# Gate gathers in front of their rows, POOL's share of the splits kept to the end, and the lists' one-hots by one comparison on the vector engine

## The chip, the cores and the metric

The kernel runs on one core of one Trainium2 chip. The metric is the device time of one execution in microseconds (us). Three timed runs of the kernel before gave 2374.19, 2374.76 and 2380.31 us; the median is 2374.76 us. The engines are named as in the profile: PE multiplies matrices (PEld is its loading of weights), DVE is the vector engine, ACT the scalar engine, POOL the GpSimd engine, which also issues all gathers by index, and SP issues plain transfers.

## The reference

One layer on 256 latent tokens and 256 context tokens of width 2048, in float32: modulated RMSNorm, one input projection, a bidirectional mLSTM and a differential attention, gated sum, output projection, residual; then a retrieval of experts, and a final RMSNorm. Only the retrieval matters here, cut to its core:

```python
def peer(h, w_pq, sub_keys, expert_u, expert_v):
    q = (h @ w_pq).reshape(B, T, P_HEADS, 2, P_KEY_DIM // 2)
    s = jnp.einsum('bthpd,hpnd->bthpn', q, sub_keys)
    s1, i1 = lax.top_k(s[..., 0, :], P_TOPK)       # 16 of 128 keys
    s2, i2 = lax.top_k(s[..., 1, :], P_TOPK)
    ...                                             # the best 16 of their 256 sums
    g = jax.nn.softmax(top_s, axis=-1)
    def block(args):                                # 16384 experts, 8 x 16 for each token
        hx, ix, gx = args
        act = jax.nn.gelu(jnp.einsum('td,ted->te', hx, expert_u[ix]))
        return jnp.einsum('te,ted->td', gx * act, expert_v[ix])
```

Each token has 8 heads of 16 experts. An expert is one row of 2048 numbers in `expert_u` and one in `expert_v`, 16384 of each (128 MB a matrix).

## The kernel before

A product in full precision is made of three products of halves. `stage` (line 126) loads a piece of 128x1024 numbers (`raw`), ACT rounds it (`hi`, line 133), and DVE or POOL subtracts (`lo`, line 136). While the flag `by_four` is set, every fourth `lo` goes to POOL and three to DVE; once the flag `alone` is set too, all go to DVE. `raw`, `hi` and `lo` have three buffers each, so a piece is made at most three ahead of its use.

The last half of the program is the retrieval. Its stages overlap:

- **The u stage.** For each of 128 columns of experts, PE multiplies the tokens with `expert_u` (`u_pair`, two columns a call). A column is two half columns, and a half column is one piece: 8 products with `hi` (512 wide) and 8 with `lo` (256 wide). DVE then adds the two halves (`act`, line 1601), ACT takes the gelu (line 1602), and the result is written to `ag_dram` (line 1606), where each expert has its activations beside its gate weights.
- **Side work.** At each half column, `pump` takes `pace[0]` steps of a generator (`plan`): the selection of experts, the map of gate weights (`gate_map`), the lists of experts by the group of tokens that uses them (`lists`), and the first row groups (`soon`). A tile scheduler puts the instructions of each engine in an order; the gathers and the matmuls of this stage keep the order of the program. Every engine works its own order through without leaving it.
- **`lists`** ends with 126 columns of places. For four columns at a time `one_hots` makes two tiles: `o1`, one-hots of the place inside a block, on ACT (an Abs for each column, a Relu for four), and `o2`, one-hots of the block times the expert's number, by four comparisons, two on DVE and two on POOL (line 1238). PE multiplies them (the matmuls `g<-o,o`) and sums 126 products in one PSUM tile. From it come `idxV` and `idxG`, the lists for the gathers.
- **The v stage.** Experts come in blocks of 128. For each block POOL gathers 128 rows of `expert_v` (`vraw`, 1 MB, `stage_rows`) and 128 rows of gates and activations from `ag_dram` (`ag`, 128 KB for one token tile, 256 KB for two, `stage_gates`); DVE multiplies gate and activation (`w`, lines 1509 and 1512). A block used by all tokens of a tile is split into `hi`, `lo` (lines 1488, 1490, 1496, 1497) and multiplied in 12 matmuls for each token tile; blocks that 32 tokens use come by fours (an item) and are multiplied unsplit, 32 columns each (`v<-vraw,w`). There are 99 gathered blocks and 2 plain ones (`DENSE`). `soon` takes the first five items of four while the u stage still runs and fetches two more; the rest are worked off after it.

Rows come in tiles of two: four tiles at first, and two more (`vex`) once the u stage has given up its memory, so 12 rows. A tile is filled again when both of its rows have been multiplied. Gates have buffers of their own, 8 of 128x256 and 4 of 128x512. `fetch_gates` issues them up to five items ahead as far as these buffers go, item by item, and `next_item` issues it before and after the rows.

Of the kernel before, what the change touches and what calls it, by code (L numbers as in the profile page):

```python
# [19 lines left out]
F32 = mybir.dt.float32  # L20
# [65 lines left out]
def build(tc, a, dump=None):  # L86
# [34 lines left out]
    rings = []  # L121

    shared = [0]
    alone = [False]

    def stage(src, ring=None):
        if ring is None:
            ring = rings.pop(0)
            rings.append(ring)
        pool, bufs = ring  # L130
        r = load(src, pool, bufs[0])
        h = pool.tile([P, 1024], F32R, name="hi", tag="hi", bufs=bufs[1])
        nc.scalar.copy(h, r)  # L133
        l = pool.tile([P, 1024], F32R, name="lo", tag="lo", bufs=bufs[2])
        shared[0] = (shared[0] + 1) % 4 if by_four[0] and not alone[0] else 1
        (nc.vector if shared[0] else nc.gpsimd).tensor_tensor(l, r, h.bitcast(F32), op=OP.subtract)  # L136
        return h, l

# [31 lines left out]
    def b3(t, n):  # L170
        return t.unsqueeze(2).to_broadcast([P, t.shape[1], n])
# [1058 lines left out]

    def one_hots(rows, cols, factor, n=4, width=P):
        o1 = gm.tile([P, 4, P], F32, name="o1", tag="o1", bufs=3)
        for i in range(n):
            nc.scalar.activation(o1[:, i], iota, AF.Abs, bias=rows[:, i:i + 1], scale=-1.0)
        nc.scalar.activation(o1[:, 0:n], o1[:, 0:n], AF.Relu, bias=ones[:, 0:1], scale=-1.0)
        o2 = gm.tile([P, 4, P], F32, name="o2", tag="o2", bufs=3)
        for i in range(n):
            (nc.gpsimd if i % 2 else nc.vector).tensor_scalar(o2[:, i, 0:width], iota[:, 0:width], cols[:, i:i + 1], factor[:, i:i + 1],  # L1238
                                    op0=OP.is_equal, op1=OP.mult)
        return o1, o2  # L1240
# [49 lines left out]
    def lists():  # L1290
# [99 lines left out]
            w = slice(i, min(i + 4, N_LIST))  # L1390
            return one_hots(hl[:, 1, w], hl[:, 0, w], number[:, w], w.stop - i, N_BLOCKS)

        pace[0] = 1.05
        ready = [hots(0)]
        yield
        ready.append(hots(4))
# [23 lines left out]
        ls.release()  # L1420
        yield

    vst = None
    pace = [1.05]

    def plan():
        nonlocal vst
        yield from retrieve(0)
        for _ in weave(gate_map(0), retrieve(1)):
            yield  # L1430
        tk.release()
        vst = tc.alloc_tile_pool(name="vst", bufs=1, side="right", reuse_waits="tile")
        yield from gate_map(1)
        while leaving:
            step(leaving)
            yield
        pace[0] = 2
        yield from lists()
        pace[0] = 1.3
        alone[0] = True  # L1440
        yield from soon()

    n = P - N_LIST + 1
# [33 lines left out]
    def stage_gates(kind, i):  # L1477
        if kind == DENSE:
            return i
        n = len(TILES[kind])  # L1480
        ag = vst.tile([P, 2 * n * P], F32, name="ag", tag=f"ag{n}", bufs=AG[n - 1])
        src = (ag_tile, ag_dram)[n - 1]
        gather(ag, src[0:2 * P * (1 + EARLY)] if kind < 8 and i < CAPS[kind] - 1 else src, idxG, BASE[kind] + i)
        return {t: ag[:, 2 * j * P:2 * (j + 1) * P] for j, t in enumerate(TILES[kind])}
# [29 lines left out]
        return out  # L1514

    FIRST_OF = [sum(len(x) for x in ITEMS[:n]) for n in range(len(ITEMS) + 1)]
    rows_in = []
    gates_in = []
    staged = [0, 0]


    AG = 8, 4
    USES = [[sum(k != DENSE and len(TILES[k]) == w for k, _ in x) for w in (1, 2)] for x in ITEMS]

    def fetch_gates(n):
        while staged[1] < (min(len(ITEMS), n + 5) if n else 1) and all(sum(u[w] for u in USES[n:staged[1] + 1]) <= AG[w] for w in range(2)):
            gates_in.append([stage_gates(*b) for b in ITEMS[staged[1]]])
            staged[1] += 1

    def next_item(n):  # L1530
        if n > 1:
            fetch_gates(n)
        while staged[0] < len(ITEMS):
            last = FIRST_OF[staged[0] + 1] - 1
            if last // 2 * 2 - 11 >= FIRST_OF[n] or vex is None and last > 7:
                break
            rows_in.append([stage_rows(*b) for b in ITEMS[staged[0]]])
            staged[0] += 1
        fetch_gates(n)
        return [(raw, weights_of(kind, ins)) for (kind, _), raw, ins in  # L1540
                zip(ITEMS[n], rows_in.pop(0), gates_in.pop(0))]

    def accumulators(t):
        pool = tc.alloc_tile_pool(name=f"psV{t}", bufs=1, space=PSUM, side=("left", "right")[t], reuse_waits="tile")
# [16 lines left out]
    def soon():  # L1561
        nonlocal psG
        psG.release()
        out_acc[0] = accumulators(0)
        work = SOON + ITEMS[:2]
        for n, item in enumerate(work):
            rows, gates = [], []
            if n == 0:
                rows = [stage_rows(*b) for b in item]
                while made[0] < EARLY:  # L1570
                    yield
            for j, b in enumerate(item):
                if n:
                    rows.append(stage_rows(*b))
                    yield
                gates.append(stage_gates(*b))
                if j == 1 and 0 < n <= len(SOON):
                    parts = [(raw, weights_of(kind, ins)) for (kind, _), raw, ins in zip(work[n - 1], *held)]
                yield
            if 0 < n <= len(SOON):  # L1580
                v_groups(0, work[n - 1], parts, first=n == 1)
                yield
            held = rows, gates
            if n >= len(SOON):
                rows_in.append(rows)
                gates_in.append(gates)
                staged[0] += 1
                staged[1] += 1

    back.append(plan())  # L1590
    pump(1)
# [56 lines left out]
    with tc.If(rest > 0):  # L1648
        with tc.For_i(0, N_LIST, 1) as i:
            col_ = av.tile([P, 1], F32, name="ocol", bufs=1)  # L1650
            nc.sync.dma_start(col_, over_dram[:, bass.ds(i, 1)])
            for t in range(2):
                ag = av.tile([P, 2 * P], F32, name="oag", bufs=1)
                nc.sync.dma_start(ag, ag_dram[bass.ds(i * P + P, P), 2 * t * P:2 * (t + 1) * P])
                w = av.tile([P, P], F32, name="ow", bufs=1)
# [53 lines left out]
            residual(t, c)  # L1709
    for t in range(2):  # L1710
        finish_tile(t)
    for p in (fn, vex, *v_pools, av, vst, tkr, gm, stg, cst, dr):
        p.release()


# [67 lines left out]
```

## Time and profile before

| | before |
|---|---|
| median of 3 runs | 2374.76 us |
| profiled execution | 2391.27 us, span 2389.6 us |
| PE busy | 2240.4 us (94%) |
| DVE, ACT, POOL busy | 1540.9, 1101.3, 904.9 us |
| granted TensorE clock, mean | 0.973 |
| u stage, first to last matmul | 1176 to 2079 us |
| the lists' one-hots | about 1792 to 1908 us |
| first row gather | 1913 us |
| v stage after the u stage | 2079 to 2366 us |

How to read it: times in rows count from the start of the span. A row in order of time gives start and length in us, engine, line, operation, the tile written and the tiles read (numbers left out), its shape, and in brackets how long the engine had been idle and what ended that. PE's rows overlap, since matmuls are pipelined: the distance of two starts is what one costs.

### The profile page before, as it was taken

Reading aid. Unit: us, or ns where it says so; the run is one execution under the profiler, and the core shown is the slowest. Engines: PE = TensorE matmul, PEld = TensorE weight load, DVE = VectorE, ACT = ScalarE, POOL = GpSimd, SP = SyncE. Lnnn points to the kernel's source line nnn. Section 1 sums busy time; section 2 is a strip of 40 time slices with the busy share of each in tenths; the row PEclk is TensorE's granted clock in tenths of the full one; section 3 lists DMA queues with packets and bytes.
Section 4 is the critical chain, followed back from the end, with each engine's and each line's share of the span. In section 5 each row is a group of like instructions: output and inputs, shape, how many; then the busy total and the mean of one; then the engine's idle time right before and its main releaser. Section 6 shows DMA issues by size and latency. Waiting matters only on the chain. (4 is left out here: it accounts for less than half of the span.)

```text
span 2389.6 us, 37883 instructions
## 1 busy us (share of the span) xinstructions
PE 2240.4 (94%) x14330; PEld 1920.6 (80%) x14330; DVE 1540.9 (64%) x2898; ACT 1101.3 (46%) x1849; POOL 904.9 (38%) x908
## 2 busy tenths in 40 slices
PE   6999999999999999999998999999999989988786
PEld 3679989998889999879987888887889967665553
DVE  3357874768866768656798667874985434444444
ACT  3232322244556644444445778973338723333332
POOL 2132211245624200002266556752227642454554
PEclk9999999999999999999999999999999999999898
DMA  9968954876546588755555578789555589886977
GB/s 380 348 203 317 322 207 167 300 206 173 150 127 196 200 280 282 254 194 165 178 178 181 176 208 221 202 224 262 174 185 170 160 330 359 333 344 253 381 299 268
DMA packets 235913, 571.02 MB, mean 239 GB/s; under 512 B 85154, under 2 KB 118739, under 8 KB 221264
## 3 DMA queue, kind: packets, MB, share of 16 engines
q1 hardware_dynamic: 153888, 339.34, 43.9%
q0 software_dynamic: 46992, 211.67, 24.7%
q10 hardware_dynamic: 34848, 17.57, 2.5%
q8 instruction: 113, 1.85, 0.3%
q14 instruction: 72, 0.59, 0.1%
HBM read 524.33 MB, written 38.93 MB: 236 GB/s over the span
## 5 line engine op out<-in xcount | busy, mean ns | idle before, releaser
L133 ACT CAST hi<-raw 128x1024 fp32r<-128x1024 f32 x528 | 552.3, 1049 | 806.0 <-PE acc L289 270.0
L136 DVE TENSOR_TENSOR lo<-raw,hi 128x1024 fp32r<-128x1024 f32 x467 | 588.8, 1265 | 268.2 <-ACT hi L133 261.6
L92 PE MATMUL s<-h,hi 128*128 128x512 f32 x2048 | 748.3, 407 | 1.7 <-ACT hi L133 1.7
L92 PE MATMUL s<-h,lo 128*128 128x256 f32 x2048 | 581.5, 284 | 30.4 <-DVE lo L136 26.1
L92 PEld LDWEIGHTS s<-h,hi 128*128 128x128 f32 x2048 | 391.1, 191 | 96.0 <-ACT hi L133 5.2
L92 PEld LDWEIGHTS s<-h,lo 128*128 128x128 f32 x2048 | 393.1, 192 | 39.3 <-DVE lo L136 31.2
L289 PE MATMUL acc<-hL,hi 128*128 128x256 f32 x2048 | 420.5, 285 | 0.0
L289 PEld LDWEIGHTS acc<-hL,hi 128*128 128x128 f32 x2048 | 339.3, 192 | 4.2 <-issue 3.9
L289 PE MATMUL acc<-hL,lo 128*128 128x256 f32 x1024 | 291.0, 285 | 3.7 <-DVE lo L136 3.7
L136 POOL TENSOR_TENSOR lo<-raw,hi 128x1024 fp32r<-128x1024 f32 x61 | 158.9, 2604 | 267.6 <-ACT hi L133 253.6
L289 PEld LDWEIGHTS acc<-hL,lo 128*128 128x128 f32 x1024 | 196.2, 192 | 5.4 <-DVE lo L136 4.5
L116 POOL DMA_DIRECT2D raw<-w_mod x128 | 68.2, 533 | 301.3 <-DVE raw L522 279.6
L522 DVE SCALAR_TENSOR_TENSOR raw<-raw,cr 128x1024 f32<-128x1024 f32 x128 | 154.6, 1219 | 34.4 <-DMA raw<-w_mod 19.2
L1238 POOL TENSOR_SCALAR o<-iota,i1T,gT 128x128 f32<-128x128 f32 x128 | 140.3, 1103 | 94.8 <-PE g L92 48.8
L1474 POOL DMA_INDIRECT vraw<-expert_v,idxV x99 | 105.1, 1062 | 176.1 <-PE v L92 101.8
L1490 DVE TENSOR_TENSOR lo<-vraw,hi 128x1024 fp32r<-128x1024 f32 x74 | 90.2, 1225 | 116.1 <-ACT hi L1488 69.1
L92 PE MATMUL v<-hi,l 128*128 128x512 f32 x448 | 129.8, 408 | 19.3 <-issue 11.4
L1488 ACT CAST hi<-vraw 128x1024 fp32r<-128x1024 f32 x74 | 77.2, 1050 | 132.5 <-PE v L92 88.3
L289 PE MATMUL acc<-hC,hi 128*128 128x256 f32 x512 | 134.0, 283 | 0.0
L1601 DVE TENSOR_REDUCE act<-s 128x256 f32<-128x512 f32 x126 | 86.5, 686 | 72.9 <-PE s L92 66.0
L1474 POOL DMA_INDIRECT ag<-ag_dram,idxG x99 | 103.4, 1045 | 64.5 <-issue 25.5
L92 PEld LDWEIGHTS v<-hi,l 128*128 128x128 f32 x448 | 87.3, 198 | 46.4 <-issue 16.8
(420 smaller groups left out, 3953.1 us busy)
## 6 DMA issues: line engine op xcount, KB each, us to landing
raw<-expert_u SPq DMA_DIRECT2D x256, 512.0 KB
raw<-w_in SPq DMA_DIRECT2D x176, 512.0 KB
raw<-w_mod POOLq DMA_DIRECT2D x128, 512.0 KB
raw<-w_mod SPq DMA_DIRECT2D x64, 512.0 KB
raw<-w_out SPq DMA_DIRECT2D x32, 512.0 KB
raw<-w_pq SPq DMA_DIRECT2D x32, 512.0 KB
ag_dram<-gates SPq DMA_DIRECT2D x32, 512.0 KB
ag_dram<-act ACTq DMA_DIRECT2D x126, 128.0 KB
```

What stands on the lines that cost most here:

```text
L92: tc.keep_in_program_order(mm(*args, **kw))
L116: d = queue.dma_start(r, src)
L133: nc.scalar.copy(h, r)
L136: (nc.vector if shared[0] else nc.gpsimd).tensor_tensor(l, r, h.bitcast(F32), op=OP.subtract)
L289: mm(acc[c][:, g * T:(g + 1) * T], lhsT=hl[sb][:, k2 * 512 + c * P:k2 * 512 + (c + 1) * P], rhs=rhs(sa, g, k), start=first and k2 == 0 and ...
L522: product = nc.vector.scalar_tensor_tensor(r, r, 1.0, cr, op0=OP.mult, op1=OP.mult, accum_out=part[:, h, i:i + 1])
L1238: (nc.gpsimd if i % 2 else nc.vector).tensor_scalar(o2[:, i, 0:width], iota[:, 0:width], cols[:, i:i + 1], factor[:, i:i + 1], op0=OP.is_e ...
L1474: tc.keep_in_program_order(nc.gpsimd.indirect_dma_start(out=out, out_offset=None, in_=src, in_offset=bass.IndirectOffsetOnAxis(ap=idx[:, b ...
L1488: nc.scalar.copy(h, raw)
L1490: nc.vector.tensor_tensor(l, raw, h.bitcast(F32), op=OP.subtract)
L1601: nc.vector.reduce_sum(act[:, e], ps.rearrange("p s t -> p t s"), axis=AX.X)
```

## The change

Four things change; the start of the program up to the lists' one-hots keeps its order.

1. `one_hots` makes the `o1` of the lists by one comparison on DVE, 128x512, in place of five instructions on ACT. The `o1` of the gate map stay on ACT.
2. The pace of that loop is 1.35 steps a half column in place of 1.05.
3. `alone` is gone: POOL makes every fourth `lo` to the end of the u stage.
4. Gates lie in one pool of 12 buffers of 128x512, and each block's gate gather is issued right in front of its row gather. `fetch_gates` and its rules are gone; rows are staged block by block. In `soon`, gates go in front of rows too, with one step of the generator for each gather.

A small tile in the branch for lists that overflow is reused as well; the branch isn't entered.

```diff
-        shared[0] = (shared[0] + 1) % 4 if by_four[0] and not alone[0] else 1
+        shared[0] = (shared[0] + 1) % 4 if by_four[0] else 1
...
+        if width < P:
+            nc.vector.tensor_tensor(o1[:, 0:n], b3(rows, P), iota.unsqueeze(1).to_broadcast([P, n, P]), op=OP.is_equal)
+        else:
+            for i in range(n):
+                nc.scalar.activation(o1[:, i], iota, AF.Abs, bias=rows[:, i:i + 1], scale=-1.0)
+            nc.scalar.activation(o1[:, 0:n], o1[:, 0:n], AF.Relu, bias=ones[:, 0:1], scale=-1.0)
...
-        pace[0] = 1.05
+        pace[0] = 1.35
...
+        gates = tc.alloc_tile_pool(name="ag", bufs=1, side="right", reuse_waits="tile")
         pace[0] = 1.3
-        alone[0] = True
...
-        ag = vst.tile([P, 2 * n * P], F32, name="ag", tag=f"ag{n}", bufs=AG[n - 1])
+        ag = gates.tile([P, 4 * P], F32, name="ag", tag="ag", bufs=12)[:, 0:2 * n * P]
...
-    def fetch_gates(n):
-        while staged[1] < (min(len(ITEMS), n + 5) if n else 1) and all(sum(u[w] for u in USES[n:staged[1] + 1]) <= AG[w] for w in range(2)):
-            gates_in.append([stage_gates(*b) for b in ITEMS[staged[1]]])
-            staged[1] += 1
...
+            b = staged[0]
+            if b // 2 * 2 - 11 >= FIRST_OF[n] or vex is None and b > 7:
                 break
-            rows_in.append([stage_rows(*b) for b in ITEMS[staged[0]]])
+            ins = stage_gates(*BLOCKS_OF[b])
+            fetched.append((stage_rows(*BLOCKS_OF[b]), ins))
             staged[0] += 1
...
             for j, b in enumerate(item):
-                if n:
-                    rows.append(stage_rows(*b))
-                    yield
-                gates.append(stage_gates(*b))
+                ins = stage_gates(*b)
+                yield
+                new.append((stage_rows(*b) if n else rows[j], ins))
```

What this does to the orders is seen in three places. First DVE near the end of the lists' one-hots, before (`o2` are the comparisons by block, `lo` the splits, `act` the sums of the u stage):

```order
L1601 TENSOR_REDUCE act_19503<-s_19353 128x256
L1238 TENSOR_SCALAR o2_19457<-iota_76,pairs_17226,number_17150 128x99 x2
L1238 TENSOR_SCALAR o2_19494<-iota_76,pairs_17226,number_17150 128x99 x2
L136 TENSOR_TENSOR lo_19470<-raw_19466,hi_19468 128x1024
L1601 TENSOR_REDUCE act_19503<-s_19428 128x256
L1238 TENSOR_SCALAR o2_19538<-iota_76,pairs_17226,number_17150 128x99 x2
```

and after:

```order
L1590 TENSOR_REDUCE act_19322<-s_19179 128x256
L1233 TENSOR_TENSOR o1_19269<-pairs_17226,iota_76 128x512
L1240 TENSOR_SCALAR o2_19271<-iota_76,pairs_17226,number_17150 128x99 x2
L1233 TENSOR_TENSOR o1_19280<-pairs_17226,iota_76 128x512
L1240 TENSOR_SCALAR o2_19282<-iota_76,pairs_17226,number_17150 128x99 x2
L135 TENSOR_TENSOR lo_19295<-raw_19291,hi_19293 128x1024
```

Each step now has a comparison of 128x512 in front of its two small ones. On PE the 32 steps stand in front of half columns 183 to 212 before and 183 to 205 after, counted along its order; the rows of the five groups of `soon` stand in front of half columns 224, 230, 237, 244 and 251 before and 222, 228, 235, 242 and 249 after.

Second, POOL in the u stage, where rows of `soon` are gathered (each `vraw` is one row block, `ag` its gates). Before:

```order
L1474 DMA vraw_19894<-expert_v,idxV_10954 128x2048
L1474 DMA ag_19973<-ag_dram_83,idxG_10955 128x256
L1474 DMA vraw_20013<-expert_v,idxV_10954 128x2048
L1474 DMA ag_20044<-ag_dram_83,idxG_10955 128x256
L1474 DMA vraw_20013<-expert_v,idxV_10954 128x2048
L1474 DMA ag_20092<-ag_dram_83,idxG_10955 128x256
L1474 DMA vraw_20102<-expert_v,idxV_10954 128x2048
```

and after:

```order
L1476 DMA ag_19845<-ag_dram_83,idxG_10955 128x256
L135 TENSOR_TENSOR lo_19852<-raw_19848,hi_19850 128x1024
L1476 DMA vraw_19870<-expert_v,idxV_10954 128x2048
L1476 DMA ag_19894<-ag_dram_83,idxG_10955 128x256
L1476 DMA vraw_19870<-expert_v,idxV_10954 128x2048
L1476 DMA ag_19934<-ag_dram_83,idxG_10955 128x256
L1476 DMA vraw_19958<-expert_v,idxV_10954 128x2048
L135 TENSOR_TENSOR lo_19965<-raw_19961,hi_19963 128x1024
L1476 DMA ag_19983<-ag_dram_83,idxG_10955 128x256
```

The gate stands in front of its row, and a `lo` stands among the gathers at every fourth half column (`lo_19852` is that of half column 224, `lo_19965` that of 228). `vraw_20013` before and `vraw_19870` after are the first tile that waits for a group of rows to be multiplied.

Third, POOL in the v stage, some 130 us into it before:

```order
L1474 DMA ag_21416<-ag_dram_83,idxG_10955 128x512
L1474 DMA ag_21418<-ag_dram_83,idxG_10955 128x512
L1474 DMA ag_21420<-ag_dram_83,idxG_10955 128x256
L1474 DMA ag_21422<-ag_dram_83,idxG_10955 128x256
L1474 DMA ag_21424<-ag_dram_83,idxG_10955 128x256
L1474 DMA ag_21426<-ag_dram_83,idxG_10955 128x256
L1474 DMA ag_21476<-ag_dram_83,idxG_10955 128x512
L1474 DMA ag_21478<-ag_dram_83,idxG_10955 128x256
L1474 DMA ag_21480<-ag_dram_83,idxG_10955 128x512
L1474 DMA ag_21482<-ag_dram_83,idxG_10955 128x256
L1474 DMA vraw_21484<-expert_v,idxV_10954 128x2048 x2
```

and in the same stage after:

```order
L1476 DMA ag_21181<-ag_dram_83,idxG_10955 128x256
L1476 DMA vraw_21183<-expert_v,idxV_10954 128x2048
L1476 DMA ag_21185<-ag_dram_83,idxG_10955 128x512
L1476 DMA vraw_21183<-expert_v,idxV_10954 128x2048
L1476 DMA ag_21258<-ag_dram_83,idxG_10955 128x256
L1476 DMA vraw_21260<-expert_v,idxV_10954 128x2048
```

Runs of up to twelve gates, behind which rows queue, have become gate and row by turns.

## Rows read from the trace of the kernel before

**Rows 1.** Windows: length, busy us of PE, PEld, DVE, ACT, POOL; PE clock, DMA share, GB/s.
```profile
1799.00:1911.00 112.00, 112.00 (x738) 101.48 (x737) 55.26 (x95) 91.74 (x185) 78.93 (x66) 1.00 0.53 161
1912.00:2080.00 168.00, 149.59 (x860) 114.72 (x862) 68.44 (x103) 48.36 (x51) 60.99 (x57) 0.94 0.89 336
...
2080.00:2170.00 90.00, 77.39 (x374) 54.88 (x367) 40.96 (x77) 30.94 (x46) 50.03 (x49) 0.91 0.92 369
2170.00:2205.00 35.00, 29.58 (x153) 21.41 (x152) 15.86 (x36) 10.50 (x16) 14.36 (x14) 0.95 0.44 160
...
2080.00:2366.00 286.00, 243.41 (x1186) 167.53 (x1182) 126.10 (x245) 91.42 (x133) 147.53 (x141) 0.92 0.84 329
...
2110.00:2120.00 10.00, 10.00 (x46) 8.28 (x45) 7.77 (x12) 5.41 (x8) 3.13 (x5) 1.00 1.01 419
```
**Rows 2.** What PE waited for, 1912 to 2080 us: sum, times, longest.
```profile
PE s L92 <- DVE lo L136: 17.8, 6, 7.5
```
**Rows 3.** DVE in order of time, where the longest of these waits ends.
```profile
1932.03 0.19 DVE L1509 TENSOR_TENSOR w<-ag 128x32 f32<-128x32 f32 x1 [2.93 <-DMA ag<-ag_dram,idxG]
...
1932.50 1.23 DVE L136 TENSOR_TENSOR lo<-raw,hi 128x1024 fp32r<-128x1024 f32 x1
```
**Rows 4.** POOL in order of time, v stage: gathers around two waits for gate buffers.
```profile
2169.52 2.08 POOL L1474 DMA_INDIRECT vraw<-expert_v,idxV  x1 [6.88 <-DVE l L1497]
...
2183.79 1.00 POOL L1474 DMA_INDIRECT ag<-ag_dram,idxG  x1 [7.61 <-DVE w L1512]
...
2195.72 1.37 POOL L1474 DMA_INDIRECT ag<-ag_dram,idxG  x1 [9.68 <-DVE w L1509]
...
2204.97 0.95 POOL L1474 DMA_INDIRECT vraw<-expert_v,idxV  x1 [0.30 <-issue]
```
**Rows 5.** PE in order of time, v stage: the matmul after that gap.
```profile
2218.47 1.22 PE L92 MATMUL v<-hi,l 128*128 128x512 f32 x2 [9.70 <-issue]
```
**Rows 6.** What PE waited for, 2080 to 2200 and 2300 to 2390 us.
```profile
PE v L92 <- DVE w L1509: 8.5, 2, 6.0
...
PE v L92 <- DVE w L1509: 8.0, 2, 7.2
```
**Rows 7.** PE in order of time: one step of the lists a half column; steady half columns; one group.
```profile
1884.57 1.03 PE L92 MATMUL g<-o,o 128*128 128x99 f32 x8
...
1888.24 1.03 PE L92 MATMUL g<-o,o 128*128 128x99 f32 x8
...
1915.07 0.28 PE L92 MATMUL s<-h,lo 128*128 128x256 f32 x1
...
1915.42 0.28 PE L92 MATMUL s<-h,lo 128*128 128x256 f32 x1
...
1957.19 3.64 PE L92 MATMUL v<-vraw,w 128*32 128x512 f32 x32
```
**Rows 8.** POOL in order of time, lists' one-hots.
```profile
1838.01 2.26 POOL L1238 TENSOR_SCALAR o<-iota,pairs,number 128x99 f32<-128x99 f32 x2 [1.48 <-issue]
1841.62 1.47 POOL L1238 TENSOR_SCALAR o<-iota,pairs,number 128x99 f32<-128x99 f32 x2 [1.35 <-PE g L92]
1843.06 2.39 POOL L136 TENSOR_TENSOR lo<-raw,hi 128x1024 fp32r<-128x1024 f32 x1
```
**Rows 9.** DVE in order of time, beside the first of these.
```profile
1838.46 1.21 DVE L136 TENSOR_TENSOR lo<-raw,hi 128x1024 fp32r<-128x1024 f32 x1
```
**Rows 10.** Groups by shape, 1680 to 1790 us: busy us, mean ns, idle before.
```profile
L136 POOL TENSOR_TENSOR lo<-raw,hi 128x1024 fp32r<-128x1024 f32 x9 | 31.5, 3502 | 87.4 <-ACT hi L133 78.1 <-DVE place L1347 9.3
L1339 DVE TENSOR_TENSOR rank<-rank,g 128x504 f32<-128x504 f32 x5 | 3.4, 679 | 0.2
```
**Rows 11.** POOL in order of time, u stage: a wait on the gathers under way, one for rows.
```profile
1931.87 0.94 POOL L1474 DMA_INDIRECT ag<-ag_dram,idxG  x1 [2.82 <-DMA vraw<-expert_v,idxV]
...
1961.10 0.94 POOL L1474 DMA_INDIRECT vraw<-expert_v,idxV  x1 [22.71 <-PE v L92]
1962.35 0.95 POOL L1474 DMA_INDIRECT ag<-ag_dram,idxG  x1 [0.30 <-issue]
```

More of the change, by code (lines that the diff above doesn't have):

```diff
@@ L123, in build @@
     shared = [0]
-    alone = [False]
     def stage(src, ring=None):
@@ L1232, in one_hots @@
         o1 = gm.tile([P, 4, P], F32, name="o1", tag="o1", bufs=3)
-        for i in range(n):
-            nc.scalar.activation(o1[:, i], iota, AF.Abs, bias=rows[:, i:i + 1], scale=-1.0)
-        nc.scalar.activation(o1[:, 0:n], o1[:, 0:n], AF.Relu, bias=ones[:, 0:1], scale=-1.0)
+        if width < P:
[4 more added lines that the diff above has]
+            nc.scalar.activation(o1[:, 0:n], o1[:, 0:n], AF.Relu, bias=ones[:, 0:1], scale=-1.0)
         o2 = gm.tile([P, 4, P], F32, name="o2", tag="o2", bufs=3)
@@ L1421, in lists @@
         yield
-    vst = None
+    vst = gates = None
     pace = [1.05]
     def plan():
-        nonlocal vst
+        nonlocal vst, gates
         yield from retrieve(0)
@@ L1516, in build @@
     FIRST_OF = [sum(len(x) for x in ITEMS[:n]) for n in range(len(ITEMS) + 1)]
[L1517 to L1523, printed above, removed]
-    def fetch_gates(n):
-        while staged[1] < (min(len(ITEMS), n + 5) if n else 1) and all(sum(u[w] for u in USES[n:staged[1] + 1]) <= AG[w] for w in range(2)):
-            gates_in.append([stage_gates(*b) for b in ITEMS[staged[1]]])
-            staged[1] += 1
-    def next_item(n):
[L1531 to L1535, printed above, removed]
+    BLOCKS_OF = [b for x in ITEMS for b in x]
+    fetched = []
+    staged = [0]
+    def next_item(n):
+        while staged[0] < len(BLOCKS_OF):
+            b = staged[0]
+            if b // 2 * 2 - 11 >= FIRST_OF[n] or vex is None and b > 7:
                 break
-            rows_in.append([stage_rows(*b) for b in ITEMS[staged[0]]])
+            ins = stage_gates(*BLOCKS_OF[b])
+            fetched.append((stage_rows(*BLOCKS_OF[b]), ins))
             staged[0] += 1
-        fetch_gates(n)
-        return [(raw, weights_of(kind, ins)) for (kind, _), raw, ins in
-                zip(ITEMS[n], rows_in.pop(0), gates_in.pop(0))]
+        return [(raw, weights_of(kind, ins)) for (kind, _), (raw, ins) in
+                zip(ITEMS[n], [fetched.pop(0) for _ in ITEMS[n]])]
     def accumulators(t):
@@ L1566, in soon @@
         for n, item in enumerate(work):
-            rows, gates = [], []
+            new = []
             if n == 0:
@@ L1572, in soon @@
             for j, b in enumerate(item):
-                if n:
-                    rows.append(stage_rows(*b))
-                    yield
-                gates.append(stage_gates(*b))
+                ins = stage_gates(*b)
+                yield
+                new.append((stage_rows(*b) if n else rows[j], ins))
                 if j == 1 and 0 < n <= len(SOON):
-                    parts = [(raw, weights_of(kind, ins)) for (kind, _), raw, ins in zip(work[n - 1], *held)]
+                    parts = [(raw, weights_of(kind, ins)) for (kind, _), (raw, ins) in zip(work[n - 1], held)]
                 yield
@@ L1582, in soon @@
                 yield
-            held = rows, gates
+            held = new
             if n >= len(SOON):
[L1585 to L1588, printed above, removed]
+                fetched.extend(new)
+                staged[0] += len(new)
     back.append(plan())
@@ L1654, in build @@
                 nc.sync.dma_start(ag, ag_dram[bass.ds(i * P + P, P), 2 * t * P:2 * (t + 1) * P])
-                w = av.tile([P, P], F32, name="ow", bufs=1)
+                w = ag[:, 0:P]
                 nc.vector.scalar_tensor_tensor(w, ag[:, 0:P], col_, ag[:, P:2 * P], op0=OP.mult, op1=OP.mult)
@@ L1711, in build @@
         finish_tile(t)
-    for p in (fn, vex, *v_pools, av, vst, tkr, gm, stg, cst, dr):
+    for p in (fn, vex, *v_pools, av, gates, vst, tkr, gm, stg, cst, dr):
         p.release()
```

## The prediction

> **What bounds the kernel now.** I read the windows by stage first, then what PE waits for in the stages that the change touches, then the orders in time of the engines that those waits name.
>
> Up to the lists the program stays as it is. In the lists' one-hots PE has no idle time: 112.00 busy of 112 at clock 1.00 [rows 1]. So there the change can only lose. From 1912 to 2080 us PE is busy 149.6 of 168 at clock 0.94 [rows 1], and of its idle time 17.8 us end with a `lo` of DVE [rows 2]. The longest of these shows why: DVE had waited 2.93 us for a gate gather, and the `lo` that PE needed stood behind the `w` that reads it [rows 3]. In the v stage, 2080 to 2366 us, the transfers move 329 GB/s on the mean, but 419 GB/s when the queues are full, and 160 GB/s from 2170 to 2205 us [rows 1]. In that last stretch no row is gathered: after the row at 2169.52 us come gates, two of which wait 7.6 and 9.7 us for a buffer that a `w` must first give back, and the next row goes at 2204.97 us [rows 4]. PE then stands 9.7 us, until 2218.47 us [rows 5]. Gates that come late to `w` cost PE at least another 8.5 and 8.0 us at other places [rows 6]. So the v stage is bound by the row transfers, and these are held up by gates ahead of them in POOL's order.
>
> **What the stages would take without such holds.** A half column of the u stage is 8 pairs of matmuls at 0.35 us (1915.07 to 1915.42), 2.80 us; with one step of the lists it is 3.67 us (1884.57 to 1888.24), so a step is 0.87; a group of rows is 3.6 us [rows 7]. From half column 213, where the lists end at 1911 us, to 256 that is 43 × 2.80 + 5 × 3.6 = 138 us; it took 168. The excess, about 29 us, is 18 of waits, and the clock: 0.94 of 168 us is 10 us lost at the lower level (1.2 of 2.4 GHz), which follows the stops. In the v stage 329 GB/s × 286 us = 94.1 MB. At the full rate, which I take as 410 GB/s, that is 230 us. PE's own work is 243.4 us at mean clock 0.92 [rows 1], about 224 us at the full clock. The two floors are nearly equal.
>
> **The change part by part.** The sum is made against the profiled execution's 2391.3 us (span 2389.6); the median of the runs is 2374.8, 16.5 us less, and I subtract that at the end.
>
> *Comparison on DVE, pace 1.35.* PE's work is the same 32 steps, spread over 23 half columns in place of 30; where the stage ends later, work after it is less by as much. So it costs nothing as long as POOL, DVE and ACT keep up. ACT loses four Abs and a Relu a step. DVE gains a comparison of 128x512; the trace doesn't show one from these operands, and the nearest row, 504 wide, takes 0.68 us [rows 10]. DVE was busy 55 of 112 us [rows 1]; 32 × 0.68 is 22 more, in 92 us. POOL is the one to watch. Its pair of comparisons takes 1.47 us alone but 2.26 beside a `lo` of DVE (POOL 1838.01, DVE 1838.46), so a 1.21 us subtraction on DVE adds 0.79, or 0.65 of its length [rows 8, 9]. A half column now gives POOL 1.35 × 1.47 = 1.98, a quarter of a `lo` at 2.39 = 0.60, and what DVE adds: three quarters of a `lo` at 0.79 = 0.59, and 1.35 comparisons at 0.65 × 0.68 = 0.60. Sum 3.77 us; PE needs 2.80 + 1.35 × 0.87 = 3.97. The cover is 0.2 us thick. Bounds: 0; and if each comparison on DVE held POOL for its length, pairs took 2.26 + 0.44 and POOL's `lo` the 3.5 us that they took beside dense DVE work [rows 10]: 1.35 × (2.70 + 0.68) + 0.88 = 5.4, 1.5 × 23 = +33 us. I take +3, near the sum from rows 8.
>
> The Trainium skill, SBUF — State Buffer, "Who interferes with whom", says that a DVE instruction with two SBUF inputs contends with a GpSimd instruction that reads SBUF, and that the loser blocks fully. The trace agrees in direction (2.26 against 1.47 us), but shows 0.79 us added by a 1.21 us instruction. By the rule in full the sum above would be 1.98 + 0.60 + 0.75 × 1.21 + 1.35 × 0.68 = 4.4 us, some 10 us lost over the stage.
>
> *`soon` earlier, gates in front, POOL's `lo` between.* Rows now start at about half column 207 instead of 214, the groups stand only 2 half columns earlier, so the first rows and gates have some 5 half columns (14 us) more. The 29 us of excess have three sources: `w` waiting for gates on DVE in front of a `lo`; bursts of four rows beside the u pieces; DVE's own order. The first is eased: a gate no longer lies behind its own row in the queue, and a quarter of the `lo` leaves DVE. The bursts stay. What POOL's `lo` waits behind: gathers. One that waits for rows to be multiplied held POOL 22.7 us, and a gather then costs 1.25 us (1961.10 to 1962.35) [rows 11]. In the new order the wait at the group in front of half column 222 is followed by five gathers and then the `lo` of 228: 3.6 + 6.3 + 2.4 = 12.3 us after the group's start, while PE needs it after 3.6 + 6 × 2.80 = 20.4. The tightest is `lo` 232 behind the wait at 228: 3.6 + 1.25 + 2.4 = 7.3 against 14.8. So the waits are hidden, by 7 to 8 us. With three buffers a split is made at most some two half columns ahead, 5.6 us, and 2.4 of these are POOL's. Bounds: all 29 gone; or none, and POOL's longer `lo` late by a microsecond at each of 12 places, +12. I take half: −14.
>
> *Gates in turn with rows in the v stage.* A gate now waits for the `w` of twelve blocks before, and the row behind it for a tile of which the older row is twelve blocks old too; `w` is done before the rows are multiplied, so the gate's wait is never the later one. Two gathers a block cost POOL 2 × 1.25 = 2.5 us; a row and its gates (1.18 to 1.31 MB) at 410 GB/s take 2.9 to 3.2. So POOL's issuing is hidden too, thinly. What is late next: the rows themselves, and where items of four need little PE time, PE waits for rows; where blocks for all tokens come, rows wait for PE. With twelve rows between two floors of 224 and 230 us neither is reached. The best stretch before, 2080 to 2170 us, ran at 369 GB/s with its own small holds [rows 1]; at that rate 94.1 MB take 255 us, 31 less than 286. Bounds: the floor of 230, −56; and nothing, 0. I take −31. The end after 2366 us is left as it is.
>
> Sum: +3 − 14 − 31 = −42. 2391.3 − 42 = 2349; less 16.5, 2333 us.
>
> **Rivals.**
>
> *Rows, not gates, set the v stage.* For it: PE's floor and the transfers' floor are near each other, so a wait taken from one is given to the other; POOL waited even for gathers under way, 2.8 us [rows 11]. Against it: the 35 us at 160 GB/s. Then about a third of each gain stays, −10 and −5, and +1 in the lists: 2361 us.
>
> *All holds vanish.* −56 − 29 + 0 = −85: 2290 us. Against it: bursts of four rows remain in the u stage.
>
> *POOL and DVE shut each other out.* In the lists POOL falls behind PE; from 3.97 us of POOL work a half column on, each 0.1 us more costs 2.3 us, because PE multiplies in order and stands. At the upper bound it loses 33 us, and in the u stage the `lo` of POOL come late, +12, with no gain there. The v stage has no `lo` on POOL and keeps its −31. Sum +14: 2389 us, slower. For it: POOL's `lo` of 3.5 us, the cover of 0.2 us; against it: the steps of 1.47 and 2.26 us. The skill's rule named above, in full in every stage, would be a weak form of this one.
>
> **How the numbers follow.** Forecast 0.61, rows set the stage 0.22, all holds vanish 0.10, POOL shut out 0.05, others 0.02. A measurement of this kernel tells about 0.3%, 7 us, from no change. Faster: 0.61 + 0.10 + most of 0.22 = 0.89. Same 0.05, from the weak end of the second case. Slower 0.06. The range 2304 to 2366 us reaches from half the way to "all holds vanish" to just past "rows set the stage"; the forecast's own range is 2313 to 2352.
>
> **What would show it.** In the profile after: no wait of a POOL gate for `w` with rows behind it; the mean rate from the end of the u stage to the last matmul at 360 to 375 GB/s, and that stretch 250 to 260 us; PE's waits for `lo` between the lists and the end of the u stage about half of 17.8 us; PE still without idle time in the lists' steps, POOL's pairs there at up to 2.7 us. The forecast is wrong if the v stage's rate stays near 329 GB/s, if PE waits at `g<-o,o`, or if POOL's `lo` are what PE waits for in the u stage.

## The result, and the profile after

The changed kernel took 2347.76 us (median of 4 runs, 2346.51 to 2352.58), the kernel before 2377.53 us in 4 runs beside it on the same chip. The ratio is 0.9878 with a 95% interval of 0.9854 to 0.9902: faster by 1.2%, about 30 us. The profiled execution took 2346.6 us (span 2344.8). Further runs follow on three chips, called A, B and C here; which chip this first result came from isn't on record, and the text calls it the first chip. A ratio is always to runs of the kernel before on the same chip, and on chip C the changed kernel gained nothing (0.9982). So there are two things to explain: the gain, and why it isn't had everywhere.

The windows of the changed kernel by stage: lists' one-hots, u stage behind them, v stage, end. Columns are as in [rows 1].

```profile
1791.00:1893.00 102.00, 102.00 (x678) 92.59 (x676) 77.31 (x138) 31.24 (x33) 89.00 (x70) 1.00 0.51 160
1893.00:2082.50 189.50, 168.50 (x965) 130.82 (x963) 73.34 (x105) 56.44 (x60) 93.18 (x68) 0.95 0.83 314
2082.50:2327.40 244.90, 228.76 (x1201) 150.79 (x1200) 130.22 (x254) 93.53 (x141) 157.40 (x145) 0.97 0.97 392
2327.40:2344.80 17.40, 0.00 (x0) 0.00 (x0) 7.85 (x14) 4.73 (x11) 6.37 (x5) 0.64 0.33 121
```

In the lists PE still has no idle time. What POOL and DVE do there, by shape from 1800 to 1893 us (busy us, mean ns of one; answers to [rows 8, 10]): POOL's comparisons by block, 1.164 us each and so a pair in 2.33 us, its `lo`, and DVE's new comparison:

```profile
L1240 POOL TENSOR_SCALAR o<-iota,pairs,number 128x99 f32<-128x99 f32 x61 | 70.4, 1164 | 2.0 <-PE g L92 1.9
L135 POOL TENSOR_TENSOR lo<-raw,hi 128x1024 fp32r<-128x1024 f32 x6 | 14.7, 2453 | 0.0
```

```profile
L1233 DVE TENSOR_TENSOR o<-pairs,iota 128x512 f32<-128x512 f32 (+1 forms) x29 | 22.3, 767 | 17.7 <-PE g L92 17.7
```

How POOL and DVE meet is seen in single comparisons of the kernel before, one beside a `lo` of DVE and one alone:

```profile
1838.76 1.50 POOL L1238 TENSOR_SCALAR o<-iota,pairs,number 128x99 f32<-128x99 f32 x1
...
1841.62 0.77 POOL L1238 TENSOR_SCALAR o<-iota,pairs,number 128x99 f32<-128x99 f32 x1 [1.35 <-PE g L92]
```

The first started inside the `lo` that ran from 1838.46 to 1839.67 us [rows 9] and ended 0.59 us after it. So it looks held until the `lo` was done, and then it took little less than a comparison takes alone.

The u stage ends at 2082.5 us; in [rows 1] it ended near 2079. The v stage moves 392 GB/s in place of 329. To see what follows from what, here is the kernel before, profiled once more on chip A, where it took 2375.1 us (span 2373.1):

```profile
1791.00:1905.00 114.00, 114.00 (x747) 103.13 (x746) 57.25 (x102) 95.25 (x197) 82.22 (x71) 1.00 0.52 163
1905.00:2074.40 169.40, 150.81 (x870) 117.16 (x873) 70.76 (x107) 49.66 (x53) 60.02 (x56) 0.95 0.88 330
2074.40:2353.00 278.60, 237.49 (x1200) 167.08 (x1200) 130.87 (x253) 94.31 (x139) 146.78 (x144) 0.93 0.88 345
2353.00:2373.00 20.00, 0.00 (x0) 0.00 (x0) 10.60 (x16) 5.50 (x13) 9.58 (x7) 0.59 0.29 105
```

Against this one the changed kernel is 8.1 us later at the end of the u stage, 33.7 us shorter in the v stage and 2.6 us shorter in the end: 28 us of span in all. Against the profile that the prediction used it is 3.8 later, 44.2 shorter (289.1 us from 2078.7 to 2367.8) and 4.4 shorter.

**The v stage.** What PE waited for, 2082 to 2328 us, and two of the groups of POOL's waits there. They answer to [rows 4 to 6]:

```profile
PE v L92 <- DMA vraw<-expert_v,idxV: 14.2, 6, 4.4
PE v L92 <- ACT hi L1490: 1.0, 1, 1.0
PE v L92 <- DVE lo L1492: 0.5, 1, 0.5
```

```profile
POOL ag L1476 <- DMA vraw<-expert_v: 11.9, 1, 11.9
POOL vraw L1476 <- DMA vraw<-expert_v,idxV: 9.5, 11, 2.7
```

No wait of PE ends with a `w` any more, and POOL has none for `w` in front of a gate. In the second profile of before, 2074 to 2353 us, the largest of these were:

```profile
PE v L92 <- DVE w L1509: 30.4, 6, 8.3
...
POOL ag L1474 <- DVE w L1509: 21.2, 4, 9.7
```

What is left is PE waiting for rows under way. The transfers then run at their limit, four windows in a row:

```profile
2110.00:2140.00 30.00, 30.00 (x183) 18.98 (x181) 12.81 (x30) 10.03 (x14) 21.76 (x22) 1.00 1.01 413
2140.00:2170.00 30.00, 29.99 (x135) 24.47 (x132) 21.89 (x40) 17.23 (x26) 21.20 (x20) 1.00 1.02 413
2170.00:2200.00 30.00, 30.00 (x171) 20.28 (x173) 15.63 (x34) 10.56 (x17) 22.05 (x20) 1.00 1.02 413
2200.00:2230.00 30.00, 30.00 (x176) 20.26 (x172) 17.53 (x36) 14.22 (x21) 21.43 (x20) 1.00 1.02 413
```

The stretch from 2170 to 2205 us ran at 160 GB/s before [rows 1]. The Trainium skill, Perfetto Trace Analysis, "Roofline", says that a core whose neighbour is idle may pull more than its share of 358 GB/s, up to about 435 GB/s for 16 DMA engines. The rows agree: 413 GB/s at a share of 1.02.

**The u stage.** What PE waited for there, which answers to [rows 2]:

```profile
PE s L92 <- POOL lo L135: 11.1, 4, 7.7
PE s L92 <- DVE lo L135: 4.9, 6, 1.8
PE s L92 <- ACT hi L132: 4.9, 3, 2.4
```

DVE's `lo` fell from 17.8 to 4.9 us, and POOL's `lo` took its place. The longest is here, POOL in order of time, then the store on ACT's queue, then PE:

```profile
1898.29 1.10 POOL L1476 DMA_INDIRECT vraw<-expert_v,idxV  x1 [1.58 <-DVE idxV L1421]
...
1902.19 1.36 POOL L1476 DMA_INDIRECT vraw<-expert_v,idxV  x1 [0.30 <-issue]
1917.57 1.18 POOL L1476 DMA_INDIRECT ag<-ag_dram,idxG  x1 [14.02 <-DMA ag_dram<-act]
1918.77 2.35 POOL L135 TENSOR_TENSOR lo<-raw,hi 128x1024 fp32r<-128x1024 f32 x1
```

```profile
1900.58 0.90 ACTq L1595 DMA_DIRECT2D ag_dram<-act  x2
```

```profile
1921.17 0.58 PE L92 MATMUL s<-h,lo 128*128 128x256 f32 x1 [7.68 <-POOL lo L135]
```

Four rows are gathered at once from 1898.3 us. The store of the last activations that the first gate may need is issued at 1900.6 us, among them, in two pieces, and they land 11.3 and 15.6 us after their issue:

```profile
DMA to landing us min/median/max: 11.3/13.4/15.6
```

The first gate waits 14.0 us for it, and a `lo` stands behind it on POOL. Before, the lists ended later, and the first gate went out behind its four rows without a wait:

```profile
1919.42 0.95 POOL L1474 DMA_INDIRECT ag<-ag_dram,idxG  x1 [0.30 <-issue]
```

### The profile page after: what moved, and what is told of

The parts are those of the page before. It is cut to its first block, busy times and chain, and to the rows that moved or that the text cites. A ratio compares the mean times of both kernels' runs of the same rounds, so it can differ in the third digit from the quotient of the medians.

```text
span 2344.8 us, 37760 instructions
## 1 busy us (share of the span) xinstructions
PE 2223.5 (95%) x14330; PEld 1902.5 (81%) x14330; DVE 1556.0 (66%) x2920; ACT 1039.3 (44%) x1691; POOL 942.3 (40%) x918
## 5 line engine op out<-in xcount | busy, mean ns | idle before, releaser
L135 DVE TENSOR_TENSOR lo<-raw,hi 128x1024 fp32r<-128x1024 f32 x457 | 578.7, 1271 | 275.2 <-ACT hi L132 274.3
L135 POOL TENSOR_TENSOR lo<-raw,hi 128x1024 fp32r<-128x1024 f32 x71 | 183.8, 2589 | 336.3 <-ACT hi L132 298.1
L1476 POOL DMA_INDIRECT ag<-ag_dram,idxG x99 | 109.9, 1110 | 54.5 <-issue 27.1
L92 PE MATMUL v<-hi,l 128*128 128x512 f32 x448 | 121.7, 391 | 0.1
L277 PE MATMUL acc<-hi,hL 128*128 128x512 f32 x320 | 111.4, 407 | 0.5 <-ACT hi L132 0.5
```

The lines of the kernel that those rows point to most:

```text
L92: tc.keep_in_program_order(mm(*args, **kw))
L277: mm(acc[ti], lhsT=lhs(sa, ti, 2 * kp + k2), rhs=hl[sb][:, k2 * 512:(k2 + 1) * 512], start=first and k2 == 0 and i == 0, stop=last and k2 ...
L1476: tc.keep_in_program_order(nc.gpsimd.indirect_dma_start(out=out, out_offset=None, in_=src, in_offset=bass.IndirectOffsetOnAxis(ap=idx[:, b ...
```

## Experiments

Twelve runs, in three groups on one chip each. Where code is cut, `...` stands for it. On chip A the kernel before took 2374.9 us (median of 15 runs), on B 2389.0 (17), on C 2385.4 (24).

**Gates alone (chip A).** The rest of the change undone, the comparison, the pace, and POOL's share after the lists:

```diff
-        shared[0] = (shared[0] + 1) % 4 if by_four[0] else 1
+        shared[0] = (shared[0] + 1) % 4 if by_four[0] and not alone[0] else 1
...
-        if width < P:
+        if False:
...
-        pace[0] = 1.35
+        pace[0] = 1.05
...
+        alone[0] = True
```

> The gates in twelve buffers in front of their rows alone: the one-hots of places stay on ACT, the pace of the lists stays 1.05, and all lo after the lists stay on DVE. Theory A (the gain lies in the v stage and behind it, about 40 and 6 us, and hangs on the gates alone; the other parts bring next to nothing, since POOL's lo behind a gate gather takes back what an earlier start gives): 2335 to 2352 us, with about 246 us from the end of the u stage to the last matmul. Theory B (the gates need the earlier start that the pace of 1.35 gives): the first rows come later, the u stage or the v stage loses 10 to 20 us against the full change: 2358 to 2368 us.

2340.6 us, ratio 0.9854 (0.9837 to 0.9870). Theory A holds: all of the gain is had with the gates alone. This edit still changes two things, the order of the gathers and the buffers (12 of one size in place of 8 and 4); no run parts them. Its u stage ends at 2079.7 us, and its v stage is

```profile
2079.70:2321.20 241.50, 226.75 (x1201) 150.47 (x1200) 129.59 (x255) 93.52 (x141) 158.47 (x144) 0.96 0.98 398
```

**All but the gates (chip A).** The kernel before with the comparison on DVE, pace 1.35, and POOL's `lo` going on:

```diff
+        if width < P:
+            nc.vector.tensor_tensor(o1[:, 0:n], b3(rows, P), iota.unsqueeze(1).to_broadcast([P, n, P]), op=OP.is_equal)
...
-        pace[0] = 1.05
+        pace[0] = 1.35
...
-        alone[0] = True
```

> The full change without its gates: the comparison on DVE, the pace of 1.35 and POOL's lo after the lists are made, the gates are fetched as before. Theory A: within 7 us of the kernel before, 2371 to 2385 us, with some 286 us from the end of the u stage to the last matmul. Theory B (the earlier start and POOL's lo carry a share of the gain): 2355 to 2366 us. Theory C (POOL's lo and the DVE comparison cost time that the gates pay for): 2385 to 2395 us.

2381.9 us, ratio 1.0034 (1.0021 to 1.0047): slower, by 7 us at the median. That is in theory A's range, at its far end; C, which sees a cost, has the direction. Its u stage ends at 2090.9 us, 16.5 later than before on this chip; its v stage is 8 us shorter:

```profile
2090.90:2361.50 270.60, 236.75 (x1200) 166.62 (x1200) 129.99 (x250) 94.53 (x139) 150.57 (x143) 0.93 0.89 350
```

What PE waited for in its u stage, 1890 to 2085 us, and one of POOL's waits, show the same store and the same `lo` as in the full change:

```profile
PE s L92 <- POOL lo L135: 14.3, 5, 9.0
```

```profile
POOL ag L1475 <- DMA ag_dram<-act: 14.3, 1, 14.3
```

**First rows in turn (chip A).** The full change, each of the first four rows behind its gate:

```diff
-                rows = [stage_rows(*b) for b in item]
...
-                new.append((stage_rows(*b) if n else rows[j], ins))
+                new.append((stage_rows(*b), ins))
```

> The full change, but the first four rows after the lists are no longer gathered at once: each goes behind its gate, in turn, as all later ones do. Theory A (the four rows at once fill the DMA engines, so that the store of the gates lands late, POOL's first gate gather waits 14 us for it and the lo behind it makes PE wait): that wait falls below 5 us, the u stage ends 8 to 16 us sooner, 2332 to 2340 us. Theory B (POOL's lo is late there whatever the rows do, since it stands behind gathers): same time as the full change, 2345 to 2351 us. Theory C (the first group's rows then land after PE needs them): PE waits 5 to 12 us for rows in front of the first group, 2350 to 2360 us.

2334.0 us, ratio 0.9824 (0.9808 to 0.9840), theory A's range. POOL's first gate, the landing of the store that it needs (issued at 1905.4 us), and PE's waits in the u stage:

```profile
1908.99 1.80 POOL L1476 DMA_INDIRECT ag<-ag_dram,idxG  x1 [7.46 <-DVE lo L135]
```

```profile
DMA to landing us min/median/max: 1.9/1.9/2.0
```

```profile
PE s L92 <- ACT hi L132: 8.4, 2, 4.9
PE s L92 <- POOL lo L135: 4.5, 3, 1.7
PE s L92 <- DVE lo L135: 1.6, 2, 1.0
```

POOL's idle time in front of the gate is 7.5 us, not under 5 as expected. But more than half of it, from 1901.5 to 1905.4 us, lies before the store was issued at all; without the four rows in front the store landed within 2.0 us, in place of 15.6, and POOL's `lo` now cost PE 4.5 in place of 11.1 us. Some of it comes back as waits for `hi`. The profiled execution, at 2343.7 us the slowest of the five, ends the u stage at 2079.6 us, only 3 earlier, and its v stage takes 244.7 us, as in the full change. So where the rest of the 14 us between the medians (2347.8 and 2334.0) comes from, no trace shows.

**The kernel before, profiled again (chip A).**

> The kernel before, unchanged, profiled once more: its first profiled execution took 16 us more than the median of its runs, while that of the changed kernel took what its runs took. Theory A (chance of one execution): 2372 to 2382 us. Theory B (the profile slows this kernel by its DMA waits): 2388 to 2394 us again.

2375.1 us: theory A, the profile costs nothing that is seen. The 2391 us of the first profile lie among the runs of before on chip C (2380.6 to 2397.1). And its view of DMA issues has no time to landing for gathers, as no profile on chips B and C has; those on chip A and the first of the changed kernel have one. So it most likely was taken on a chip like B or C; the trace doesn't name its chip.

**POOL's lo and the early start apart (chip B).** Four kernels. The full change with all `lo` on DVE after the lists:

```diff
-        shared[0] = (shared[0] + 1) % 4 if by_four[0] else 1
+        shared[0] = (shared[0] + 1) % 4 if by_four[0] and not alone[0] else 1
...
+        alone[0] = True
```

> The full change, but after the lists all lo stay on DVE as before (POOL's share ends with the lists). The gates alone ran 7 us faster than the full change; this run and the next split these 7 us. Theory A (POOL's lo after the lists stand behind gather calls that wait, and that is the loss): no wait of PE for a lo of POOL is left, 2336 to 2342 us. Theory B (the loss is the earlier start: the first gates are asked for before the store of the pair that ends at 104 columns has landed, whoever makes the lo): 2345 to 2351 us, with a wait of PE of 5 us or more for a lo of DVE or for hi near 1920 us.

The gates with POOL's `lo`, but one-hots on ACT and pace 1.05:

```diff
-        if width < P:
+        if False:
...
-        pace[0] = 1.35
+        pace[0] = 1.05
```

> The full change, but the one-hots of places stay on ACT and the pace of the lists stays 1.05, so that the lists end near 1911 us as before; POOL's share of the lo goes on to the end. Theory A of the run above: 2345 to 2351 us, since POOL's lo still stand behind gathers. Theory B: 2337 to 2343 us, since the store has long landed when the first gate is asked for.

The gates alone, and with them the first rows in turn (against the gates alone):

```diff
-                rows = [stage_rows(*b) for b in item]
...
-                new.append((stage_rows(*b) if n else rows[j], ins))
+                new.append((stage_rows(*b), ins))
```

> The gates alone, with the first four rows behind their gates in turn. In the full change that edit was worth 14 us by the medians (2347.8 to 2334.0). Theory B above (what the edit cured is the wait for the store behind a burst of rows): here the store has landed before, so the edit does little: 2336 to 2343 us. Theory C (what it cures is the burst of four rows beside the u pieces as such): it gains here as well, 2325 to 2333 us.

The full change with the first rows in turn and all `lo` on DVE, the edits of the first and the third together:

> The full change with the first four rows behind their gates in turn and with all lo on DVE after the lists: the earlier start, without the burst and without POOL's lo. With these lo on POOL it took 2334.0 us. Theory A (POOL's lo cost time in any order): 2326 to 2331 us. Theory B (they cost only where they stand behind a gate that waits for the store): 2331 to 2338 us.

The times, in this order, are 2371.0, 2353.5, 2356.5 and 2368.8 us. The kernel before is slower on this chip too, so the ranges above, which were made for chip A, have to be read as shares of it. The ratios are 0.9933 (0.9909 to 0.9957), 0.9848 (0.9821 to 0.9874), 0.9870 (0.9848 to 0.9893), 0.9918 (0.9891 to 0.9946). The two with pace 1.05 came out near theory B: no loss from POOL's `lo` is seen when the store has landed (the first gate of the second kernel goes out after 0.30 us), and the rows in turn gain nothing that is seen. But neither has the kernel that differs from it by that one edit beside it on chip B. What this chip does pair is the early start, with the comparison that comes with it: between the third and the fourth, both with rows in turn and all `lo` on DVE, it costs 0.0048, and the two intervals just touch.

The two with pace 1.35 fit no theory by their times. In the first of them the gate waits for the store as in the full change, though no `lo` of POOL stands behind it:

```profile
1917.72 1.13 POOL L1478 DMA_INDIRECT ag<-ag_dram,idxG  x1 [14.13 <-DMA ag_dram<-act]
```

Their u stages end at 2087.9 and 2080.4 us, about where they end with POOL's `lo` (2086.8 and 2080.1 on chip C); with pace 1.05 they ended at 2069.6 and 2078.2. What they lose against the full change on the first chip is mostly in the v stage:

```profile
2087.90:2363.00 275.10, 238.64 (x1201) 156.10 (x1200) 122.65 (x245) 90.09 (x133) 152.78 (x142) 0.93 0.87 342
```

```profile
2080.40:2359.60 279.20, 238.60 (x1201) 155.34 (x1200) 122.34 (x245) 90.21 (x133) 152.61 (x142) 0.93 0.86 337
```

In both PE stood at the branch over the loop for lists that overflow. The waits of the first, 2080 to 2390 us:

```profile
PE v L92 <- PEq L1639: 11.1, 1, 11.1
```

**Side by side, and that branch (chip C).** The full change, the gates alone, and the first rows in turn were run again. The fourth kernel is the full change with `lo` on DVE and one small matmul issued five times more, since in the two kernels that stood at the branch PE's queue had one record fewer in the trace than in the full change:

```diff
...
-            mm(pc[:, 2 * s:2 * s + 2], ...)
+            for again in range(6 if k == 0 and s == 0 else 1):
+                mm(pc[:, 2 * s:2 * s + 2], ...)
```

> The changed kernel, unchanged, as the measure for the three runs beside it on the same chip: a ratio of 0.986 to 0.990 to the kernel before, as at first (0.9878).

> The gates alone once more, beside the full change on one chip. Theory B (the earlier start costs some 7 us, because the first gates are asked for before the store has landed): a ratio 0.002 to 0.004 below that of the full change. Rival (the 7 us were a difference of chips): within 0.0015 of it.

> The full change with the first four rows behind their gates, once more, beside the full change on one chip. Theory B: a ratio 0.004 to 0.007 below that of the full change, and the lowest of this call. Rival (a difference of chips): within 0.0015 of it.

> The full change with all lo on DVE after the lists, and one small matmul of the first stage issued five times more, where PE waits for weights (nothing else changes). Without the five, this kernel took a ratio of 0.9933; in its profile PE's branch over the loop for overflowing lists took 14.1 us (2109.7 to 2123.8) in place of 3.6 us, and the v stage 275 us in place of 245. Theory L (where the branch falls in PE's instructions decides; with five matmuls more it falls where it does in a kernel in which it took 3.6 us): the branch takes 3 to 4 us, ratio 0.985 to 0.989. Theory D (the lo on DVE make the v stage slower, and the branch is a symptom): the branch takes 14 us again, ratio 0.992 to 0.995.

The full change had a ratio of 0.9982 (0.9959 to 1.0006): not the gain of before. The gates alone had 0.9890 (0.9862 to 0.9919), the first rows in turn 0.9935 (0.9909 to 0.9960), the fourth 0.9991 (0.9970 to 1.0012). The gates alone and the rows in turn both stand below the full change, as theory B has it, and the rival, a mere difference of chips, falls. But the gates alone are the lowest, where theory B had the rows in turn, and what the gates alone leave out costs more here: 22 us between the medians of the first two. The gain of the full change seen at first isn't had on this chip. In the full change, on this chip, the v stage took 281.7 us:

```profile
2110.00:2140.00 30.00, 17.28 (x60) 12.94 (x59) 8.46 (x16) 7.07 (x11) 19.50 (x19) 0.81 1.01 412
2140.00:2170.00 30.00, 30.00 (x178) 18.82 (x178) 13.50 (x33) 8.45 (x13) 11.35 (x12) 0.96 0.58 219
2170.00:2200.00 30.00, 17.36 (x48) 11.30 (x47) 9.09 (x17) 8.00 (x12) 16.90 (x17) 0.72 1.01 412
2200.00:2230.00 30.00, 30.00 (x165) 20.71 (x165) 16.47 (x36) 12.34 (x19) 12.51 (x12) 1.00 0.52 183
```

These are the same four windows as above. Transfers and PE take turns: while rows come at full rate PE stands for them, and its clock falls; then PE multiplies what came, and POOL can't gather, for the tiles are taken (waits of 2087 to 2368 us):

```profile
POOL vraw L1476 <- PE v L92: 33.4, 5, 10.9
...
POOL vraw L1476 <- DVE w L1511: 18.0, 3, 9.2
```

On the first chip the first of these was 3.4 us and the second 1.7. PE is also held longer at the branch over the loop for overflowing lists, 8.1 us in place of 3.6. Its queue there, on the first chip and on C (the branch, then the next instruction):

```profile
L1637 PEldq COMPARE_BRANCH  x1: 231/231/231, 2103.9 to 2103.9; - x1
...
L1637 PEldq EVENT_SEMAPHORE  x1: 51/51/51, 2107.5 to 2107.5; - x1
```

```profile
L1637 PEldq COMPARE_BRANCH  x1: 231/231/231, 2109.9 to 2109.9; - x1
...
L1637 PEldq EVENT_SEMAPHORE  x1: 51/51/51, 2118.0 to 2118.0; - x1
```

Over all kernels with the new gates, each by its one profiled execution:

| kernel (chip) | profiled, us | its runs: median (lowest to highest) | branch, us | v stage, us |
|---|---|---|---|---|
| full change (first) | 2346.6 | 2347.8 (2346.5 to 2352.6) | 3.6 | 244.9 |
| gates alone (A) | 2340.3 | 2340.6 (2337.1 to 2341.1) | 3.6 | 241.5 |
| rows in turn (A) | 2343.7 | 2334.0 (2327.7 to 2343.7) | 3.6 | 244.7 |
| gates with POOL's `lo` (B) | 2358.3 | 2353.5 (2340.4 to 2362.9) | 3.7 | 261.7 |
| gates in turn (B) | 2358.8 | 2356.5 (2352.1 to 2366.7) | 3.6 | 255.8 |
| gates alone (C) | 2347.3 | 2360.3 (2347.3 to 2370.4) | 3.6 | 251.0 |
| rows in turn (C) | 2363.3 | 2371.7 (2360.5 to 2377.9) | 3.7 | 258.5 |
| full change (C) | 2391.6 | 2382.5 (2370.5 to 2398.7) | 8.1 | 281.7 |
| the same with five matmuls and `lo` on DVE (C) | 2388.9 | 2385.0 (2372.1 to 2394.4) | 9.2 | 276.1 |
| `lo` on DVE (B) | 2389.2 | 2371.0 (2355.5 to 2389.2) | 14.1 | 275.1 |
| `lo` on DVE and rows in turn (B) | 2384.7 | 2368.8 (2359.7 to 2384.7) | 14.2 | 279.2 |

Wherever the branch takes long, the v stage takes 275 us or more. But these are single executions: the two with 14 us were the slowest of their kernels, 18 and 16 us above the median, and the gates alone on C were the fastest of six. So it isn't shown that the long stop belongs to a kernel and not to an execution, and the medians are the better measure of the kernels. Theory L falls: the full change took 8.1 us there with its branch where it had been, and the five matmuls helped nothing. Theory D's ratio isn't met either, since on this chip the full change alone is already at 0.9982.

Nor is it shown that the stop starts the taking of turns. Against it speaks that on chip C PE's next stop, 8.1 us until 2136.2 us, came although POOL had put its gathers out since 2096.4 us with at most 0.72 us between two, so nothing that PE held had kept these rows back. What holds PE at the branch, why the rows come late, and why it is seen only with pace 1.35 and only on chips B and C, stays open.

## Why the prediction was right, and where it was not

*What bounds the v stage* was right. The gates alone give the whole gain, PE's waits for `w` are gone, and the transfers run at 413 GB/s where the stage is steady.

*The v stage's term*, −31, was too small in size: −33.7 against the profile of chip A, −44.2 against the one it was made from. I took the best stretch before, 369 GB/s, as what would be had; it was 392 GB/s over the stage.

*The lists*, +3 from a sum of 3.77 us of POOL's work against PE's 3.97: right in that POOL keeps up. PE has no idle time there, and POOL was busy 85.1 of 93 us, which at 3.97 us a half column is 3.6. The one-hots of places took 0.77 us each on DVE, where I took 0.68. One reading in the sum was wrong: the 0.79 us that a `lo` added to a pair aren't 0.65 of its length, as of a weaker block. They are near what was left of the `lo`, 0.91 us, when POOL's comparison began. So these rows agree with an exclusive lock on the shared ports, as the Trainium skill has it (SBUF — State Buffer, "Who interferes with whom"); what they don't show is the 4.4 us a half column that I worked out from it, for that sum charged POOL with every instruction of DVE in full.

*The u stage's term*, −14, failed. With the lists' +3 the end of the u stage was forecast 11 us earlier; it came 3.8 or 8.1 later. That is inside the bounds of −29 and +12 but on the other side of nothing. The step that failed is "The tightest is `lo` 232 behind the wait at 228": it looked only at waits for rows to be multiplied. The first gate waits for the store of activations, which an earlier start brings to within 14 us, and it holds the `lo` behind it. That was named as what would make the forecast wrong ("if POOL's `lo` are what PE waits for in the u stage"), and it is so, for 11.1 us; with DVE's 4.9 the waits for `lo` were 16.0 us, not half of 17.8. POOL's share of `lo` as such shows no cost: with pace 1.05 the ratio was 0.9848 with it (chip B) and 0.9854 without (chip A). The early start brings the wait: 14 us of it are there in all kernels with pace 1.35 that gather the four rows at once, whoever makes the `lo`, and in none with pace 1.05. The comparison on DVE was never run apart from the pace.

*The end*, left as it is, gave 2.6 to 4.4 us: a small term that I didn't look for.

*"Less 16.5"* was wrong. The profile of before wasn't slow by being a profile, but most likely by its chip. The changed kernel's profile equals its runs. The forecast of 2349 us for the profile came out at 2346.6, that of 2333 for the median at 2347.8, off by the term that had no cause behind it. The agreement of the first number is luck in good part: the u stage's miss of 15 us (3.8 against −11) was paid by 13 more in the v stage and 4 in the end, and on chip C, whose runs of before are like that first profile, the same kernel takes 2382.5 us. A slip beside it: 2304 us, the low end of the range, is two thirds of the way from 2333 to 2290, not half.

*Rivals.* "Rows set the v stage" has a share in it: PE now waits 14.2 us for rows. "POOL and DVE shut each other out" happens for single instructions, but costs PE nothing in the lists.

Of the kernels tried, the one with the first rows in turn has the lowest ratio (0.9824 on A), and on C, where both ran, it beats the full change (0.9935 against 0.9982). The gates alone are the best on C and gain 1.1% or more on both chips that they ran on; they are the version to keep.

## What to carry to other kernels

When a step is moved ahead, list for each instruction that it issues what it reads, down to the stores that must land first, and look at what stands behind it in its queue: here one wait of 14 us on a store held a subtraction that PE needed. Where a bundle of edits is made, measure the edit that the profile points to by itself: it gave all, and the others cost 7 us on chip A (without the gates) and 22 on chip C (with them). Before a profile is read as its kernel, see where its time lies among the kernel's runs. A difference between a profile and the runs is not a constant to subtract, as long as nothing shows what it is; take the profile again on the chip of the runs.

## What was not expected of the hardware

The changed kernel took 2347.8 us in the first result and 2382.5 on chip C, while the kernel before took 2377.5 and 2385.4. A stop of 8 to 14 us at a branch over a loop that isn't run went with a v stage 13 to 31 us longer than in the kernels beside it on the same chip; what is cause there isn't shown. A store of 256 KB in two pieces, issued among four gathers of 1 MB, landed 11.3 and 15.6 us after its issue, and within 2.0 us when the gathers stood behind it. And a comparison of POOL that began while a `lo` of DVE ran ended 0.59 us after that `lo`, in 1.50 us in place of 0.77.
